# Layer 0 of a two-layer trunk on one core: the norm's factor moved from the tokens to the results, half of a gate product split, later norm tokens, equal address differences

## The chip, the cores and the metric

One Trainium2 chip, one core. The time is device microseconds of one execution, the median over the runs shown. The core's engines are TensorE (PE in the rows; its weight loads are PEld), VectorE (DVE), ScalarE (ACT), GpSimd (POOL) and SyncE (SP), which issues the loads.

## The reference, cut to what matters

`x` is 256 tokens of 1024 float32. Each layer normalizes the tokens, forms one wide projection, feeds branches of width 512, multiplies each with a SiLU gate and adds an output projection to `x`. Layer 0, which the change is about:

```python
h = x * rsqrt(mean(x*x) + EPS) * norm_g[0]             # per token
u_val, u_gate, z_a, q_b, k_b, v_b, z_b = split(h @ e_w_in[0])   # 7 x 512 columns
y_a = conformer_conv(u_val, u_gate, ...) * silu(z_a)   # gated, 31 causal taps, LayerNorm, silu
q = rmsnorm(heads(q_b)); k = rmsnorm(heads(k_b)); v = heads(v_b)
y_b = moba_attention(q, k, v) * silu(z_b)
x = x + concat(y_a, y_b) @ w_out[0]
```

Layer 1 has two other attention branches (c and d) of the same form. The factor rsqrt(...) is one number per token, so it can be multiplied onto the tokens ahead of a product or onto the product's result. A later RMSNorm over a head cancels it but for its EPS.

## The kernel before, in words

A product with fp32 precision is made of three fp32r products: weights and tokens are each split into a high half (`hi`, `hhi`; a cast, mostly on ACT) and a low half (`lo`, `hlo`; the difference, on VectorE, some on POOL), and `mm3` adds hi x hi, hi x lo and lo x hi in one bank. Weights come in quarters of 256 rows (`load_w`: one load, one `hi`, one `lo` of 128 x 1024 each). `proj_chan` puts output channels on the partitions (256 tokens in a row): ug, uv, zb, za, and in layer 1 cc, zc, zd. `proj_tok` puts tokens there (512 columns in a row): qb, kb, vb and others. The first of all products, ug (the convolution's gate), is not split: whole fp32 weights times `h32` (x transposed, times norm_g, not yet the factor), in two passes each.

Layer 0 goes like this. x^T comes in pieces (`h`), is scaled by norm_g, and the ug product starts on it. x itself comes as two blocks of 128 tokens; `first_block` sums the squares, takes the factor by a power on POOL (`rsx`), makes a diagonal (`dg`), and a matmul with ones (`ps_r`) turns it into a row over all partitions (`rb`). `ht` is the scaled x^T, `hhi` and `hlo` its halves. The gate is sg = tanh(ug x rb / 2), and hc = (sg + 1) x uv is the convolution's input. VectorE adds its 31 taps for four groups of channels in turn in two banks (`acc_m`, `acc_o`; 31 x 4 operations), the last of each giving `ya`. `ps_y` transposes `ya` for the LayerNorm, `ps_n` transposes it back. Beside this run the q, k and v products, the attention, and the gates zb and za (`silu2`: tanh on ACT, then z on VectorE). `po` is the output projection with weights `hi_o`, `lo_o`.

No loop sets the order. A Recorder collects every instruction (all of them bear line L384, so rows are told apart by tile names), and `issue` sorts them by the time at which inputs and engine are free, then by the rank of their stage in the table ORDER, then within the stage; for `copy` and `minus` it also picks the engine. Each engine runs its list strictly in order. Loads go out on SP in program order.

## Time and profile before

| | |
|---|---|
| median of 3 runs | 270.2 us (269.99 to 270.39) |
| the profiled execution | 270.53 us, its span 268.5 us |
| granted TensorE clock | 1.0 in each stretch read here |
| busy: PE, DVE, ACT, POOL | 260.0, 197.1, 172.3, 108.0 us |

A row of the timeline gives start, duration, engine, instruction (output<-inputs), and in brackets the idle time of the engine ahead of it with what ended it. Rows of one group run on ("x24" is 24 instructions). Instructions of one engine overlap: the distance of starts, not the duration, is what one costs. In the table by stretch each engine has its busy time and, in brackets, its number of instructions, then come the clock (1.00 is the full level), the DMA share and GB/s.

### The profile page before, as it was taken

How to read it: one execution, taken by the hardware profiler on the slowest of the kernel's cores; microseconds unless marked ns; L12 is line 12 of the kernel's file. 1: busy time of each engine (PE TensorE's matmuls, PEld its weight loads, DVE VectorE, ACT ScalarE, POOL GpSimd, SP SyncE). 2: the span in 40 equal slices, each digit the busy share in tenths (PEclk: the TensorE clock that was granted, in tenths of full speed). 3: DMA queues.
4: the chain of work that ended last, by engine and by line, in shares of the span. 5: the costliest groups of instructions: out<-in, count | busy, mean ns of one | idle time of the engine just before them, and what ended most of it. 6: DMA issues, size and time to landing. Idle time of an engine off the chain costs nothing.

```text
span 268.5 us, 5004 instructions
## 1 busy us (share of the span) xinstructions
PE 260.0 (97%) x1693; PEld 212.4 (79%) x1693; DVE 197.1 (73%) x511; ACT 172.3 (64%) x458; POOL 108.0 (40%) x143
## 2 busy tenths in 40 slices
PE   7889999999999999999899999999999999999994
PEld 5679987878789988878679879678878987667684
DVE  1399999999999999458987213589979856765231
ACT  2267779799995656656467223688869768775300
POOL 0100019858735923202424474154991420545000
PEclk9999999999999999999999999999999999999999
DMA  6998987725763445301858827498885200000031
GB/s 198 361 386 286 354 279 279 212 101 160 236 193 121 171 147 145 89 0 40 282 158 221 231 67 250 160 343 254 273 289 149 86 4 0 2 0 1 2 117 39
DMA packets 28072, 44.89 MB, mean 167 GB/s; under 512 B 3344, under 2 KB 10256, under 8 KB 28048
## 3 DMA queue, kind: packets, MB, share of 16 engines
q1 hardware_dynamic: 28048, 44.58, 50.9%
q8 instruction: 13, 0.21, 0.3%
q14 instruction: 11, 0.09, 0.1%
HBM read 43.26 MB, written 1.05 MB: 165 GB/s over the span
## 4 chain that ended last, share of the span: by engine, by line
PE 61%; DVE 13%; DMA 12%; ACT 5%; POOL 3%; issue 3%; SPq 2%; DVEq 0%; POOLq 0%; ACTq 0%
PE po L384 15%; PE pj_zd L384 5%; PE pj_vb L384 4%; PE pj_za L384 4%; PE pj_zb L384 4%; PE pj_qc L384 4%; PE pj_kv L384 4%; DMA h<-in_prm_dram 3%; PE po_c L384 3%; DMA raw_o<-in_w_out_dram 3%; DMA raw_qd<-in_o_w_in_dram 2%; SPq L384 2%; DMA raw_kb<-in_e_w_in_dram 2%; PE pj_cc L384 2%; PE pt_c L384 2%
## 5 line engine op out<-in xcount | busy, mean ns | idle before, releaser
L384 POOL TENSOR_SCALAR p_c<-p_c,r_c 128x128 f32<-128x128 f32 (+1 forms) x32 | 19.5, 625 | 27.1 <-ACT th_zd L384 8.9
L384 DVE SCALAR_TENSOR_TENSOR acc_m<-hc,cw,acc_m 128x256 f32<-128x256 f32 x58 | 28.0, 483 | 0.2
L384 DVE SCALAR_TENSOR_TENSOR acc_o<-hc,cw,acc_o 128x256 f32<-128x256 f32 x58 | 28.1, 484 | 0.0
L384 PE MATMUL po<-hi_o,yh 128*128 128x512 f32 (+1 forms) x72 | 27.0, 382 | 0.0
L384 PE MATMUL po<-hi_o,yl 128*128 128x512 f32 (+1 forms) x72 | 27.0, 379 | 0.0
L384 PE MATMUL po<-lo_o,yh 128*128 128x512 f32 (+1 forms) x72 | 26.8, 374 | 0.0
L384 POOL TENSOR_TENSOR lo_vb<-raw_vb,hi_vb 128x1024 fp32r<-128x1024 f32 x4 | 9.5, 2409 | 25.7 <-ACT hi_vb L384 25.7
L384 ACT CAST hi_o<-raw_o 128x1024 fp32r<-128x1024 f32 x16 | 16.4, 1045 | 3.4 <-DMA raw_o<-in_w_out_dram 1.6
L384 DVE TENSOR_TENSOR lo_o<-raw_o,hi_o 128x1024 fp32r<-128x1024 f32 x13 | 15.7, 1213 | 1.5 <-ACT hi_o L384 1.5
L384 PE MATMUL pj_ug<-h,raw_ug 128*128 128x256 f32 x64 | 15.4, 392 | 1.4 <-DMA raw_ug<-in_e_w_in_dram 1.4
L384 PEld LDWEIGHTS po<-hi_o,yl 128*128 128x128 f32 x72 | 13.5, 188 | 2.9 <-issue 0.7
L384 ACT ACTIVATE p_c<-sn,mn_c 128x256 f32<-128x256 f32 (+1 forms) x32 | 14.3, 450 | 2.2 <-DVE mn_c L384 2.2
L384 PEld LDWEIGHTS po<-hi_o,yh 128*128 128x128 f32 x72 | 13.6, 189 | 2.7 <-issue 0.3
L384 PEld LDWEIGHTS pj_ug<-h,raw_ug 128*128 128x128 f32 x64 | 12.2, 197 | 3.8 <-issue 2.3
L384 PEld LDWEIGHTS po<-lo_o,yh 128*128 128x128 f32 x72 | 13.6, 188 | 1.9
L384 POOL TENSOR_TENSOR rsx<-ssx,mhalf 128x1 f32<-128x1 f32 x4 | 2.7, 680 | 27.0 <-DVE ssx L384 27.0
L384 DVE TENSOR_TENSOR x<-x,po 128x512 f32<-128x512 f32 (+1 forms) x9 | 5.6, 625 | 8.6 <-PE po L384 8.6
L384 DVE CUSTOM_DVE_ANT_0 sn<-s_c,shp 128x256 f32<-128x256 f32 (+1 forms) x32 | 10.7, 349 | 1.6 <-ACT p_c L384 0.9
L384 POOL TENSOR_TENSOR lo_o<-raw_o,hi_o 128x1024 fp32r<-128x1024 f32 x3 | 7.2, 2417 | 7.0 <-ACT hi_o L384 7.0
L384 PE MATMUL pj_zd<-hlo,hi_zd 128*128 128x256 f32 x32 | 9.4, 295 | 0.0
L384 POOL TENSOR_SCALAR p_b<-p_b,r_b 128x128 f32<-128x128 f32 (+1 forms) x16 | 8.6, 555 | 1.9 <-DVE r_b L384 1.5
L384 PE MATMUL pj_zc<-hhi,lo_zc 128*128 128x256 f32 x32 | 9.2, 287 | 0.2 <-DVE lo_zc L384 0.2
(334 smaller groups left out, 916.5 us busy)
## 6 DMA issues: line engine op xcount, KB each, us to landing
raw_o<-in_w_out_dram SPq DMA_DIRECT2D x16, 512.0 KB, 5.1
raw_uv<-in_e_w_in_dram SPq DMA_DIRECT2D x4, 512.0 KB, 8.3
raw_qb<-in_e_w_in_dram SPq DMA_DIRECT2D x4, 512.0 KB, 5.4
raw_kb<-in_e_w_in_dram SPq DMA_DIRECT2D x4, 512.0 KB, 5.8
raw_vb<-in_e_w_in_dram SPq DMA_DIRECT2D x4, 512.0 KB, 4.7
raw_zb<-in_e_w_in_dram SPq DMA_DIRECT2D x4, 512.0 KB, 4.5
raw_za<-in_e_w_in_dram SPq DMA_DIRECT2D x4, 512.0 KB, 3.6
raw_kv<-in_o_w_in_dram SPq DMA_DIRECT2D x4, 512.0 KB, 3.7
```

The lines of the kernel that those rows point to most:

```text
L384: getattr(self.real[e], method)(*args, **kw)
```

## The change

Layer 0's products take unscaled tokens: `hhi` and `hlo` are the halves of x^T x norm_g, made from eight pieces of 256 columns as these come, and `ht`, the big multiplication by `rb`, is gone. `rb` is multiplied onto results: sg gets a second operation (tanh + 1) x rb, zb and za a multiplication by `rb` ahead of the tanh. In q and k the factor is left in and the head norm's EPS is scaled (`tok`, two small POOL operations per block of tokens); v is scaled by `tok` in its copy. The second half of ug (input rows 512 to 1023) is done with split weights like all others. x's two blocks are loaded after the first uv quarter instead of ahead of h4-7 and the second half of ug. All split tiles get pitches such that the two operands of a product start at equal distances modulo 256 bytes. And ORDER is another table of the same kind.

```diff
...
-ORDER = ["attc 11", "attb 0", "w kv 0", "za 3", "uv", "w uv 1", "pvd 0", "w zd 1", "o1 10", "pvc 31", "pvc 11",
+ORDER = ["w kv 1", "ug", "kd 0", "ln 2", "vb 0", "attd 0", "attb 1", "qd 0", "qd 1", "ln", "zb 1", "norm1 1",
...
-SHIFT = 8
+SHIFT = 48
+CHANNEL_MAJOR = ("uv", "zb", "za", "cc", "zc", "zd")
...
-            whole = name == "ug"
+            whole = name == "ug" and q < 2
             if whole:
-                if q % 2 == 0:
-                    both = act.tile([P, 4, 512], F32, tag=("yh", "yl")[q // 2], name=f"raw_{name}{q}")
+                if q == 0:
+                    both = act.tile([P, 4, 512], F32, tag="yh", name=f"raw_{name}{q}")
...
             if name == "ug" and q == 2:
+                load_xt(4, 4)
+            if name == "uv" and q == 1:
                 for b in range(NB):
...
-                load_xt(4, 4)
...
-            hi = wts.tile([P, 2, 512 + SHIFT], F32R, tag="hi", bufs=PARTS, name=f"hi_{name}{q}")
-            lo = wts.tile([P, 2, 512 + SHIFT], F32R, tag="lo", bufs=PARTS, name=f"lo_{name}{q}")
+            at = SHIFT if name in CHANNEL_MAJOR else 0
+            hi, lo = (wts.tile([P, 1088], F32R, tag=t, bufs=PARTS, name=f"{t}_{name}{q}")[:, at:at + 1024]
+                      .rearrange("p (c f) -> p c f", c=2) for t in ("hi", "lo"))
...
-    def rstd_of(ss, n, scale, name):
+    def rstd_of(ss, n, scale, name, eps=EPS):
...
-        nc.gpsimd.tensor_scalar(out=ms[:p_, :n], in0=ss, scalar1=scale, scalar2=EPS, op0=OP.mult, op1=OP.add)
+        nc.gpsimd.tensor_scalar(out=ms[:p_, :n], in0=ss, scalar1=scale, scalar2=eps, op0=OP.mult, op1=OP.add)
         rs = work.tile([P, 16], F32, tag="rs", name=f"rs_{name}")
...
-    hhi = act.tile([P, KC, S + SHIFT], F32R, name="hhi")[:, :, :S]
-    hlo = act.tile([P, KC, S + SHIFT], F32R, name="hlo")[:, :, :S]
+    hhi = act.tile([P, KC, S], F32R, name="hhi")
+    hlo = act.tile([P, KC, S], F32R, name="hlo")
...
-        return rs
+        return ss[:, 0:1], rs
...
-    hall = gh[:, KC:].rearrange("p (c t) -> p c t", c=KC)
+    tok = [work.tile([P, 2], F32, tag="tok", name=f"tok{b}") for b in range(NB)]
...
     def first_block(b):
...
-        t = slice(b * P, (b + 1) * P)
-        rs = square_sum(b, f"0{b}", ht)
+        ss, rs = square_sum(b, f"0{b}", ht)
...
         nc.tensor.matmul(pr[:, :P], ones, dg, start=True, stop=True)
-        nc.copy(rb[:, t], pr[:, :P])
-        h = ht.rearrange("p q (c t) -> p (q c) t", c=4)
-        nc.stage(f"norm0 r{b}")
-        kw = dict(out=h, in0=hall[:, :, t], in1=rb[:, None, t].to_broadcast([P, KC, P]), op=OP.mult)
-        nc.record(("DVE", "tensor_tensor", (), kw), ("POOL", "tensor_tensor", (), kw), kind="minus")
-        nc.copy(hhi[:, :, t], h)
-        nc.minus(hlo[:, :, t], h, hhi[:, :, t].bitcast(F32))
+        nc.copy(rb[:, b * P:(b + 1) * P], pr[:, :P])
+        nc.gpsimd.tensor_scalar(out=tok[b][:, 0:1], in0=rs, scalar1=ROOT, scalar2=None, op0=OP.mult)
+        nc.gpsimd.tensor_scalar(out=tok[b][:, 1:2], in0=ss, scalar1=EPS / D, scalar2=None, op0=OP.mult)
...
-        rs = square_sum(b, f"1{b}", ht)
+        _, rs = square_sum(b, f"1{b}", ht)
         for q in range(2):
...
             if lo is None:
-                nc.tensor.matmul(ps[:, :S], hi[:, k % 2, f], h32[k], start=k == 0, stop=k == KC - 1)
+                nc.tensor.matmul(ps[:, :S], hi[:, k % 2, f], h32[k], start=k == 0, stop=False)
...
-    def silu2(ps, dst, name):
+    def silu2(ps, dst, name, by=None):
...
         t = work.tile([P, S], F32, tag="tanh", bufs=2, name=f"th_{name}")
-        nc.scalar.activation(t, ps[:, :S], AF.Tanh, scale=0.5)
-        nc.vector.scalar_tensor_tensor(out=dst, in0=t, scalar=1.0, in1=ps[:, :S], op0=OP.add, op1=OP.mult)
+        z = ps[:, :S]
+        if by is not None:
+            nc.vector.tensor_tensor(out=dst, in0=z, in1=by, op=OP.mult)
+            z = dst
+        nc.scalar.activation(t, z, AF.Tanh, scale=0.5)
+        nc.vector.scalar_tensor_tensor(out=dst, in0=t, scalar=1.0, in1=z, op0=OP.add, op1=OP.mult)
...
-    def head_rstd(ps, nh, name):
+    def head_rstd(ps, nh, name, eps=EPS):
...
-            return rstd_of(ss[:, :nh], nh, 1.0 / HD, name)
+            return rstd_of(ss[:, :nh], nh, 1.0 / HD, name, eps)
...
-        return rstd_of(ss[:, :nh], nh, 1.0 / HD, name)
-    def head_norm(ps, name):
+        return rstd_of(ss[:, :nh], nh, 1.0 / HD, name, eps)
+    def head_norm(ps, name, eps=EPS):
...
-        rs = head_rstd(ps, NH, name)
+        rs = head_rstd(ps, NH, name, eps)
         if name[:2] in HEADS_ON_ACT:
...
-        qn = work.tile([P, 256], F32, tag="qd2", bufs=2, name=f"qn_{name}")
+        qn = work.tile([P, 256], F32, tag="tanh", bufs=2, name=f"qn_{name}")
...
     for c in range(KC):
-        nc.either(h32[c], h32[c], ng[:, c:c + 1])
+        by = ng[:, c:c + 1]
+        if c < 4:
+            nc.either(h32[c], h32[c], by)
+        else:
+            nc.scalar.mul(hhi[:, c], h32[c], by)
+            nc.vector.scalar_tensor_tensor(out=hlo[:, c], in0=h32[c], scalar=by, in1=hhi[:, c].bitcast(F32), op0=OP.mult,
+                                           op1=OP.subtract)
+    nc.stage("norm0 g1")
+    for c in range(4):
+        nc.copy(hhi[:, c], h32[c])
+        nc.minus(hlo[:, c], h32[c], hhi[:, c].bitcast(F32))
+    wuv = load_w("uv", [cols_of(0, 0, 512)])
     for b in range(NB):
...
     for m in range(4):
+        nc.stage("ug")
         ps = proj_chan(w, m, "ug")
...
+        nc.vector.scalar_tensor_tensor(out=sg[:, m], in0=sg[:, m], scalar=1.0, in1=rb, op0=OP.add, op1=OP.mult)
...
-    w = load_w("uv", [cols_of(0, 0, 512)])
     for m in range(4):
-        ps = proj_chan(w, m, "uv")
-        nc.vector.scalar_tensor_tensor(out=hc[:, m, PADC:], in0=sg[:, m], scalar=1.0, in1=ps[:, :S],
-                                       op0=OP.add, op1=OP.mult)
+        ps = proj_chan(wuv, m, "uv")
+        nc.vector.tensor_tensor(out=hc[:, m, PADC:], in0=sg[:, m], in1=ps[:, :S], op=OP.mult)
...
-        qn.append(head_norm(proj_tok(w, b, 512, "qb"), f"qb{b}"))
+        qn.append(head_norm(proj_tok(w, b, 512, "qb"), f"qb{b}", tok[b][:, 1:2]))
     w = load_w("kb", [cols_of(0, 2048, 512)])
...
-        kn.append(head_norm(proj_tok(w, b, 512, "kb"), f"kb{b}"))
+        kn.append(head_norm(proj_tok(w, b, 512, "kb"), f"kb{b}", tok[b][:, 1:2]))
...
         ps = proj_tok(w, b, 512, "vb")
-        nc.copy(v0[:, b], ps)
+        nc.scaled(v0[:, b], ps, tok[b][:, 0:1])
...
-        silu2(proj_chan(w, m, "zb"), z[:, 4 + m], f"zb{m}")
+        silu2(proj_chan(w, m, "zb"), z[:, 4 + m], f"zb{m}", rb)
     w = load_w("za", [cols_of(0, 1024, 512)])
...
-        silu2(proj_chan(w, m, "za"), z[:, m], f"za{m}")
+        silu2(proj_chan(w, m, "za"), z[:, m], f"za{m}", rb)
...
-    vcb = act.tile([P, NH, HD], F32, name="vcb")
+    vcb = work.tile([P, NH, HD], F32, tag="qk", name="vcb")
...
```

The order of VectorE around the gate products sg and the uv weights' low halves, first in the kernel before (`sg`, `hlo`, `lo_uv` as above, the rest are small constants):

```order
L384 TENSOR_TENSOR sg_206<-pj_ug_4_108,rb_177 128x256
L384 TENSOR_TENSOR sg_206<-pj_ug_5_115,rb_177 128x256
L384 TENSOR_SCALAR q_c_qnorm_g_213<-shp_121,prm_118 128x4
L384 TENSOR_SCALAR gcmp_215<-shp_121,prm_118 128x4
L384 TENSOR_SCALAR q_d_qnorm_g_217<-shp_121,prm_118 128x4
L384 TENSOR_TENSOR hlo_199<-ht_9_159,hhi_186 128x8x128
L384 TENSOR_TENSOR sg_206<-pj_ug_6_130,rb_177 128x256
L384 TENSOR_TENSOR lo_uv_2_232<-raw_uv_1_123,hi_uv_1_210 128x2x512
L384 TENSOR_TENSOR lo_uv_4_241<-raw_uv_2_128,hi_uv_3_226 128x2x512
L384 TENSOR_TENSOR sg_206<-pj_ug_7_137,rb_177 128x256
L384 TENSOR_TENSOR lo_uv_6_259<-raw_uv_3_132,hi_uv_5_238 128x2x512
L384 TENSOR_TENSOR lo_uv_8_274<-raw_uv_4_135,hi_uv_7_251 128x2x512
```

And in the changed kernel:

```order
L384 TENSOR_TENSOR sg_280<-pj_ug_4_112,rb_261 128x256
L384 TENSOR_TENSOR sg_280<-pj_ug_6_137,rb_261 128x256
L384 TENSOR_TENSOR sg_280<-pj_ug_5_119,rb_261 128x256
L384 SCALAR_TENSOR_TENSOR sg_280<-sg_280,rb_261 128x256
L384 TENSOR_TENSOR sg_280<-pj_ug_7_147,rb_261 128x256
L384 SCALAR_TENSOR_TENSOR sg_280<-sg_280,rb_261 128x256 x3
L384 TENSOR_SCALAR q_b_qnorm_g_315<-shp_140,prm_135 128x4
L384 TENSOR_SCALAR q_c_qnorm_g_318<-shp_140,prm_135 128x4
L384 TENSOR_SCALAR gcmp_321<-shp_140,prm_135 128x4
L384 TENSOR_SCALAR q_d_qnorm_g_324<-shp_140,prm_135 128x4
L384 TENSOR_TENSOR lo_uv_10_327<-raw_uv_5_130,hi_uv_9_268 128x1024
L384 TENSOR_TENSOR lo_uv_12_337<-raw_uv_6_184,hi_uv_11_306 128x1024
```

In the first list two low halves of uv (`lo_uv_2`, `lo_uv_4`) stand between gate products, and the third (`lo_uv_6`) follows the last gate product. In the second the third low half (`lo_uv_10`) comes behind eight gate operations and four constants; `hlo` is made far ahead.

The order of TensorE where the convolution's output is transposed (`ps_y`), before:

```order
L384 MATMUL pj_za_26_1235<-hhi_186,lo_za_46_921 128x256
L384 MATMUL pj_za_26_1235<-hhi_186,hi_za_45_902 128x256
L384 MATMUL po_58_1338<-hi_o_61_1325,yh_15_1193 128x512
L384 MATMUL po_59_1341<-hi_o_61_1325,yh_15_1193 128x512
L384 MATMUL ps_y_52_1343<-ident_110,ya_1129 128x128
L384 MATMUL pj_za_26_1235<-hlo_199,hi_za_45_902 128x256
L384 MATMUL pj_za_26_1235<-hhi_186,lo_za_46_921 128x256
L384 MATMUL ps_y_52_1343<-ident_110,ya_1129 128x128 x3
L384 MATMUL ps_y_53_1356<-ident_110,ya_1129 128x128 x4
L384 MATMUL pj_za_26_1235<-hhi_186,hi_za_47_924 128x256
```

And in the changed kernel:

```order
L384 MATMUL po_59_1404<-hi_o_65_1381,yl_15_1073 128x512
L384 MATMUL po_59_1404<-hi_o_65_1381,yh_14_1065 128x512
L384 MATMUL po_59_1404<-lo_o_66_1396,yh_14_1065 128x512
L384 MATMUL po_59_1404<-hi_o_65_1381,yl_15_1073 128x512
L384 MATMUL ps_y_52_1429<-ident_125,ya_1206 128x128
L384 MATMUL ps_y_53_1432<-ident_125,ya_1206 128x128
L384 MATMUL po_59_1404<-hi_o_67_1394,yh_14_1065 128x512
L384 MATMUL ps_y_52_1429<-ident_125,ya_1206 128x128
L384 MATMUL ps_y_53_1432<-ident_125,ya_1206 128x128
L384 MATMUL ps_y_52_1429<-ident_125,ya_1206 128x128
```

Before, products of the third piece of za stand around and behind `ps_y`; in the changed order they are all done and output products (`po`) stand ahead of it.

The order of VectorE ahead of the last `ya`, before:

```order
L384 SCALAR_TENSOR_TENSOR acc_m_310<-hc_87,cw_191,acc_m_310 128x256 x4
L384 SCALAR_TENSOR_TENSOR z_14_873<-th_za_35_1277,pj_za_27_1238 128x256
L384 SCALAR_TENSOR_TENSOR acc_m_310<-hc_87,cw_191,acc_m_310 128x256 x3
L384 SCALAR_TENSOR_TENSOR y_b_87_1307<-po_b_51_1294,z_14_873 128x256
L384 TENSOR_TENSOR lo_o_60_1314<-raw_o_30_1005,hi_o_59_1299 128x2x512
L384 TENSOR_TENSOR yl_16_1217<-y_b_87_1307,yh_15_1193 128x256
L384 SCALAR_TENSOR_TENSOR ya_1129<-hc_87,cw_191,acc_m_310 128x256 x2
L384 SCALAR_TENSOR_TENSOR y_b_74_1345<-po_b_45_1320,z_14_873 128x256
```

And in the changed kernel:

```order
L384 SCALAR_TENSOR_TENSOR acc_m_374<-hc_79,cw_270,acc_m_374 128x256 x2
L384 SCALAR_TENSOR_TENSOR y_b_76_1341<-po_b_45_1323,z_13_971 128x256
L384 SCALAR_TENSOR_TENSOR acc_m_374<-hc_79,cw_270,acc_m_374 128x256 x3
L384 SCALAR_TENSOR_TENSOR z_13_971<-th_za_35_1328,z_13_971 128x256
L384 TENSOR_TENSOR lo_o_64_1374<-raw_o_32_1000,hi_o_63_1353 128x1024
L384 SCALAR_TENSOR_TENSOR acc_m_374<-hc_79,cw_270,acc_m_374 128x256
L384 TENSOR_TENSOR lo_o_66_1396<-raw_o_33_1135,hi_o_65_1381 128x1024
L384 SCALAR_TENSOR_TENSOR acc_m_374<-hc_79,cw_270,acc_m_374 128x256
L384 SCALAR_TENSOR_TENSOR y_b_89_1418<-po_b_51_1386,z_13_971 128x256
L384 SCALAR_TENSOR_TENSOR ya_1206<-hc_79,cw_270,acc_m_374 128x256 x2
L384 TENSOR_TENSOR z_13_971<-pj_za_27_1336,rb_261 128x256
L384 TENSOR_TENSOR z_13_971<-pj_za_26_1269,rb_261 128x256
```

The multiplication z<-pj_za,rb is new, and two `lo_o` stand close ahead of `ya`, where there was one, with `yl` gone from there and two further multiplications z<-pj_za,rb behind it.

## Rows read from the trace of the kernel before

**Rows 1.** The page, part 1: busy time and share of each engine.

```profile
PE 260.0 (97%) x1693; PEld 212.4 (79%) x1693; DVE 197.1 (73%) x511; ACT 172.3 (64%) x458; POOL 108.0 (40%) x143
```

**Rows 2.** Busy time of each engine by stretch, busy time with instruction count, PE to POOL.

```profile
13.50:34.00 20.50, 19.49 (x133) 18.10 (x134) 19.49 (x35) 15.49 (x23) 0.41 (x1) 1.00 0.97 342
...
80.00:103.00 23.00, 23.00 (x194) 20.69 (x193) 22.69 (x62) 13.71 (x33) 12.21 (x17) 1.00 0.40 134
103.00:124.00 21.00, 21.00 (x106) 16.99 (x105) 14.00 (x31) 12.89 (x23) 4.54 (x6) 1.00 0.26 75
...
200.00:268.50 68.50, 65.08 (x489) 51.79 (x487) 39.64 (x146) 39.72 (x126) 18.94 (x41) 1.00 0.12 42
```

**Rows 3.** Waits of DVE, 13.5 to 103.2 us: us, times, longest.

```profile
DVE lo_qb L384 <- ACT hi_qb L384: 0.5, 2, 0.3
DVE ht L384 <- ACT rb L384: 0.4, 1, 0.4
DVE h L384 <- DMA h<-in_prm_dram: 0.4, 1, 0.4
```

**Rows 4.** Timeline around the convolution's end: start, us, engine, instruction, idle time before.

```profile
90.82 0.19 PEld L384 LDWEIGHTS pj_za<-hhi,hi_za 128*128 128x128 f32 x1 [0.17 <-issue]
...
91.40 0.41 DVE L384 SCALAR_TENSOR_TENSOR z<-th_za,pj_za 128x256 f32<-128x256 f32 x1
...
91.73 0.42 DVE L384 SCALAR_TENSOR_TENSOR y_b<-po_b,z 128x256 f32<-128x256 f32 x1
...
100.88 1.23 DVE L384 TENSOR_TENSOR lo_o<-raw_o,hi_o 128x1024 fp32r<-128x1024 f32 x1
...
102.02 0.42 DVE L384 TENSOR_TENSOR yl<-y_b,yh 128x256 fp32r<-128x256 f32 x1
...
102.35 0.86 DVE L384 SCALAR_TENSOR_TENSOR ya<-hc,cw,acc_m 128x256 f32<-128x256 f32 x2
...
103.13 0.27 PE L384 MATMUL ps_y<-ident,ya 128*128 128x128 f32 x1
```

**Rows 5.** Timeline of the start, and one small POOL operation from later.

```profile
9.71 3.69 PE L384 MATMUL pj_ug<-h,raw_ug 128*128 128x256 f32 x16 [0.93 <-DMA raw_ug<-in_e_w_in_dram]
...
10.88 0.69 DVE L384 CUSTOM_DVE_ANT_0 ht<-x 128x512 f32<-128x512 f32 x1 [3.26 <-DMA x<-in_x_dram]
...
12.19 0.69 DVE L384 CUSTOM_DVE_ANT_0 ht<-x 128x512 f32<-128x512 f32 x1 [0.34 <-DMA x<-in_x_dram]
...
13.23 0.67 POOL L384 TENSOR_TENSOR rsx<-ssx,mhalf 128x1 f32<-128x1 f32 x1 [0.73 <-DVE ssx L384]
...
14.15 0.49 PE L384 MATMUL ps_r<-dg,ones 128*128 128x128 f32 x2 [0.75 <-DVE dg L384]
14.27 0.28 DVE L384 TENSOR_SCALAR dg<-ident,rsx 128x128 f32<-128x128 f32 x1
...
14.99 0.49 PE L384 MATMUL ps_r<-dg,ones 128*128 128x128 f32 x2 [0.35 <-ACT rb L384]
...
15.32 5.34 PE L384 MATMUL pj_ug<-h,raw_ug 128*128 128x256 f32 x24
15.52 0.27 ACT L384 COPY rb<-ps_r 128x128 f32<-128x128 f32 x1 [0.58 <-PE ps_r L384]
...
18.92 0.76 DVE L384 TENSOR_TENSOR sg<-pj_ug,rb 128x256 f32<-128x256 f32 x2
...
24.05 2.35 DVE L384 TENSOR_TENSOR lo_uv<-raw_uv,hi_uv 128x1024 fp32r<-128x1024 f32 x2
...
51.19 0.20 POOL L384 TENSOR_SCALAR ms_qb<-ss_qb 128x8 f32<-128x8 f32 x1
```

**Rows 6.** The chain that ended last, in order of time: start, us, work.

```profile
81.31 5.29 PE pj_zb L384 x43
...
95.30 2.94 PE pj_za L384 x25
...
148.92 11.15 PE pj_qc L384 x48
```

22 rows, old and new, of the table ORDER are left out of this document.

## The prediction

> **What bounds the kernel now.** I read the page first. TensorE is busy 97% of the 268.5 us span and VectorE 73% [rows 1], so at first sight TensorE alone sets the time and whatever shortens its list is a gain. The second view, busy time by stretch, corrects this: VectorE's 73% is an average of full and idle stretches. From 13.5 to 103 us VectorE is as full as TensorE (19.49 of the first 20.5 us, still 22.69 of the last 23), and only from 103 on does it have room (14.00 of 21) [rows 2]. The third view, VectorE's waits from 13.5 to 103.2 us, shows three short ones, 1.3 us in 90 [rows 3]. So in layer 0 VectorE never rests: it writes the low halves of the split weights and adds up the 31 taps of the convolution, and the end of that, the two `ya` at 102.35 to 103.21 us, is where the convolution's output can be transposed (ps_y, 103.13 us on TensorE) and normalized [rows 4]. In the kernel before both engines reach that point together: one `ps_y` starts at 103.13 with no idle time shown ahead of it. Two lines of work therefore end there, and the later one decides. Behind it TensorE alone carries the rest: 21.00 of 21 us up to 124.
>
> The profiled execution took 270.53 us, 2.0 more than its span; the median shown is 270.2. I work out a difference in the span and add it to the median.
>
> **VectorE's line, its start.** The change orders the loads otherwise: after the second ug quarter come h4-7, two ug quarters and the first uv quarter, and only then the two halves of x. The trace has x at 10.88 and 12.19, so 1.31 us for 512 KB, and the ug quarter at 9.71 [rows 5]. Six such loads later x1 is there at 9.71 + 6 x 1.31 = 17.6 us (before: 12.19). From x1's arrival to the start of its power on POOL took 1.04 us (12.19 to 13.23). In the new order VectorE sums both blocks before either power can start, so both powers (0.67 each) stand one behind the other, with two new small scale operations (`tok`) between them. The power on one column takes 0.67 and another scale operation on a few columns, `ms_qb`, 0.20 [rows 5]; the two tok cost 0.4 by the nearer row, 1.3 by the farther. That makes 17.6 + 1.2 + 0.67 + 0.4 + 0.67 = 20.5, where 1.2 is the 1.04 and a second addition of 0.16. From the diagonal (14.27) to the factor row `rb` being copied (15.52 + 0.27) took 1.5 us, which makes about 22.0. Then VectorE scales the gate products: four multiplications and four new (tanh + 1) x rb, 8 x 0.38 (two took 0.76) = 3.0. Eight small constants from prm and shp stand ahead of them and behind them, most of 4 columns; the nearest row, a diagonal of 128 columns at 0.28, would make 2.2 of them, and I take 0.8. That is 22.0 + 3.0 + 0.8 = 25.8 us. Only behind all of these does the list have the third uv quarter's low half; it started at 24.05 before [rows 5]. So VectorE is 1.75 us late there. Bounds: 24.05, if x's later arrival cost nothing, and 26.7 with tok at the farther row. TensorE is stopped behind the same row (it has done 28 uv products by then), but that stop costs only what TensorE cannot recover before `ps_y`.
>
> **VectorE's line, from there to `ya`.** Counted in the order of both kernels, between the third uv low half and `ya`: six multiplications z<-pj,rb are new (four for zb, two for za ahead of the point), one z product less, one y_b more, one yl less, and five lo_o stand ahead instead of three. A 256-column operation here takes 0.33 (91.40 to 91.73) and a lo_o 1.14 (100.88 to 102.02) [rows 4]. 5 x 0.33 + 2 x 1.14 = 3.9 us. Nothing hides this, because VectorE has no idle time to fill [rows 3]. If the two lo_o were moved at no cost (they are done anyway, later, where VectorE has room) it is still 1.65. So `ya` ends 1.75 + 3.9 = 5.65 us later, at 108.9; bounds 105 and 110.5.
>
> **TensorE's line.** The gate product: 32 fp32 passes at 0.2225 (5.34 / 24) become 48 split products at 0.118 [rows 5, 6]: 7.1 less 5.7 = -1.4. The waits on the factor's diagonal and copy, 0.75 and 0.35 [rows 5], go, since both now stand behind all gate products. Against it the stop at the third uv quarter: TensorE reaches it about 2.5 us before its low half is written. Eight za products and five output products stand ahead of `ps_y` instead of behind it: 8 x 0.118 + 5 x 0.232 = 2.1. So TensorE comes to `ps_y` at about 103.1 - 1.4 - 1.1 + 2.5 + 2.1 = 105.2, and waits there for VectorE until 108.9. Behind the point it has 2.1 less to do.
>
> **What follows `ps_y`.** Layer 1 has the same instructions in another order. Instructions of TensorE that carry a wait fall from 174 to 163 there. One that carries a wait starts with 0.17 us idle ahead of it that the trace puts down to issue [rows 4]: between 0 and 11 x 0.17 = 1.9; I take 1.3, since some of these waits coincide with a change of shape that costs the same. The reordering itself can give or cost: TensorE's idle time from 200 us on is 3.4 of 68.5 [rows 2], the output's tail in it, and the stretches before have little, so 1.5 us either way, taken as nothing. VectorE's hlo and norm work behind the point is unchanged.
>
> **Equal address differences.** The trace does not show an address as such. Bounds: 256-column products run at 5.29 / 43 = 0.123 and 2.94 / 25 = 0.1176, 512-column ones at 11.15 / 48 = 0.232 [rows 6]. Of the first 240 stand behind the point, of the second some 350; the spread of the first would be 1.3 us if it were all addresses, and below the best rows nothing is seen. I take 1 ns for a 256-column and 1 ns for a 512-column product, 0.6 us behind the point; ahead of it a shorter TensorE only waits longer. [...]
>
> **Sum.** +5.65 - 2.1 - 1.3 - 0.6 = +1.65 us: span 270.2, and 270.2 + 1.65 = 271.9 for the time. Its own range, from the bounds above, is 270 to 273.5.
>
> **Rivals.**
> TensorE alone decides: VectorE's end is not what `ps_y` waits for, because the planner has other work to put there or VectorE's new operations overlap more than 0.33 each. For it: 97% busy and the common arrival at 103. Against: 1.3 us of VectorE waits in 90. Time: 270.2 - 1.4 - 1.1 - 1.3 - 1.0 (addresses over the whole span) = 265.4 without the uv stop, 267.9 with all of it. I take 266.5: faster.
>
> Mostly given back: `ya` is late only by the 1.65 and some 2 us at the start (the lo_o go behind other work, tok costs nothing), about 3.7 in all; less 2.1, 1.3 and 0.6 it is -0.3, 269.9. For it: the same numbers at their lower bounds.
>
> Addresses do more: the change of pitch brings products clearly below the best rows. [...]
>
> Worse: the uv stop delays hc and with it the convolution's taps, and layer 1's order costs its 1.5: +3 to +4, 273.7.
>
> **How the numbers follow.** A measurement of this kernel can tell 0.2%, 0.54 us, from no change. Forecast 0.52 (slower 0.45, same 0.07); mostly given back 0.18 (faster 0.08, same 0.10); TensorE alone 0.15, faster; addresses 0.07, faster; worse 0.08, slower. Faster 0.30, same 0.17, slower 0.53. The range 266.6 to 273.7 leaves out about half of the TensorE rival and half of the worst case.
>
> **What would show it.** Right: the third uv low half starts near 25.8 and TensorE idles 2 us or more ahead of a pj_uv; `ya` ends near 109; a `ps_y` has idle time released by VectorE; VectorE's waits up to there stay near 1 us. Wrong: `ya` before 106, or no idle time ahead of `ps_y`; rows of pj_zc, po or qc clearly under 0.1176 or 0.232; `rb` copied before 20 us.

## The result, and the profile after

The changed kernel takes 277.99 us (275.1 to 279.26), the kernel before 270.29 on the same chip: a ratio of 1.0262, interval 1.0225 to 1.0299. Forecast were 271.9 us and a range of 266.6 to 273.7: the direction held, the size did not, +7.7 us for +1.7. The profiled execution took 278.9 us. Ratios, and from here on medians, leave out executions over 1.5% above the fastest of their kernel: 279.26 here, which leaves a median of 277.08, and one each of e1, e2 and e8, which the recorded expectations still count (276.6 for e2).

The page of the changed kernel, part 1 [rows 1], and busy time by stretch in the same columns as [rows 2]; the last row begins at its first `ps_y`:

```profile
PE 262.1 (95%) x1709; PEld 214.5 (77%) x1709; DVE 203.5 (73%) x528; ACT 173.9 (63%) x464; POOL 111.4 (40%) x146
```

```profile
13.50:34.00 20.50, 18.56 (x146) 17.69 (x145) 18.89 (x40) 14.99 (x23) 3.00 (x6) 1.00 0.94 320
80.00:103.00 23.00, 19.74 (x164) 17.60 (x165) 23.00 (x60) 11.64 (x29) 8.01 (x14) 1.00 0.51 161
103.00:124.00 21.00, 21.00 (x134) 17.64 (x133) 16.88 (x44) 14.60 (x32) 8.45 (x13) 1.00 0.27 77
...
112.50:276.90 164.40, 158.02 (x1069) 126.78 (x1067) 104.80 (x291) 94.48 (x245) 65.32 (x96) 1.00 0.40 128
```

For the last row, the same stretch of the kernel before, from its first `ps_y` to the end:

```profile
103.10:268.50 165.40, 160.42 (x1082) 129.08 (x1080) 105.86 (x289) 97.41 (x246) 63.88 (x97) 1.00 0.41 130
```

VectorE is now full from 80 to 103 us (23.00 of 23), and TensorE, full there before, idles 3.3 us. The loss lies ahead of `ps_y`: it starts at 112.50 for 103.13 [rows 4], 9.4 us later. Behind it only 1.0 of the 4.0 us forecast came back (165.4 to 164.4): TensorE is busy 2.4 less with 13 products fewer, about the moved work, and idle 1.4 more.

The start, changed kernel, timeline [rows 5]:

```profile
16.06 0.63 ACT L384 ACTIVATE ht<-x 128x512 f32<-128x512 f32 x1 [0.23 <-DMA x<-in_x_dram]
...
17.38 0.63 ACT L384 ACTIVATE ht<-x 128x512 f32<-128x512 f32 x1 [0.59 <-DMA x<-in_x_dram]
...
21.62 0.27 ACT L384 COPY rb<-ps_r 128x128 f32<-128x128 f32 x1
...
22.01 1.08 DVE L384 TENSOR_TENSOR sg<-pj_ug,rb 128x256 f32<-128x256 f32 x3
...
22.48 0.39 PE L384 MATMUL pj_uv<-hhi,hi_uv 128*128 128x256 f32 x1 [1.16 <-DVE sg L384]
...
25.21 2.34 DVE L384 TENSOR_TENSOR lo_uv<-raw_uv,hi_uv 128x1024 fp32r<-128x1024 f32 x2
```

x1 lands at 17.38 (forecast 17.6), `rb` is written at 21.9 (22.0), the third uv low half starts at 25.21 (25.8; before 24.05). What I had not seen is the 1.16 us of TensorE at 22.48: the first uv product goes into a bank from which `sg` has yet to be read. TensorE's stop at a uv low half, forecast at 2.5 us, came to 0.4. Around the convolution's end [rows 4], changed kernel:

```profile
92.69 2.50 POOL L384 TENSOR_TENSOR lo_o<-raw_o,hi_o 128x1024 fp32r<-128x1024 f32 x1 [8.83 <-ACT hi_o L384]
92.90 2.58 DVE L384 SCALAR_TENSOR_TENSOR z<-th_zb,z 128x256 f32<-128x256 f32 x1
...
96.26 0.39 PE L384 MATMUL pj_za<-hhi,hi_za 128*128 128x256 f32 x1 [2.60 <-DVE z L384]
...
111.65 0.86 DVE L384 SCALAR_TENSOR_TENSOR ya<-hc,cw,acc_m 128x256 f32<-128x256 f32 x2
...
112.50 0.38 PE L384 MATMUL ps_y<-ident,ya 128*128 128x128 f32 x2
```

A product of 256 columns takes 2.58 us where its like took 0.41 [rows 4]. It ends just after GpSimd's `lo_o` does (95.48 and 95.19), and TensorE waits 2.60 us behind it. Ahead of `ps_y` itself no idle time is shown. Before, `z<-th_zb,pj_zb` had one input in SBUF and one in PSUM; now the factor is multiplied on first and both inputs, `th_zb` and `z`, are in SBUF. The kernel before had the same neighbours and no stall, as its timeline shows (the first row is two `lo_o`, 2.4 us each):

```profile
85.52 4.80 POOL L384 TENSOR_TENSOR lo_o<-raw_o,hi_o 128x1024 fp32r<-128x1024 f32 x2 [2.32 <-ACT hi_o L384]
...
89.46 0.42 DVE L384 SCALAR_TENSOR_TENSOR z<-th_zb,pj_zb 128x256 f32<-128x256 f32 x1
```

Side by side: the product with both inputs in SBUF takes 2.58 us beside a `lo_o` of 2.50 and ends 0.29 behind it, and the one with an input in PSUM takes 0.42 beside the 4.80. My reading of these rows, put to the test in e8 and e10, was that the first waits out GpSimd's `lo_o`, whose two inputs (`raw_o`, `hi_o`) are in SBUF as well.

VectorE's waits from 25 to 112.5 us [rows 3], and the granted clock (third number from the end) around TensorE's wait of 2.01 us for `qn_qb` at 47.22, both of this execution:

```profile
DVE lo_zb L384 <- ACT hi_zb L384: 2.5, 1, 2.5
DVE acc_o L384 <- ACT acc_o L384: 0.7, 1, 0.7
```

```profile
46.00:48.00 2.00, 0.78 (x5) 0.60 (x5) 2.00 (x6) 1.43 (x6) 2.00 (x2) 0.94 0.63 230
48.00:50.00 2.00, 2.00 (x7) 1.62 (x6) 2.00 (x6) 2.00 (x5) 2.00 (x2) 0.50 0.00 1
50.00:52.00 2.00, 2.00 (x8) 1.57 (x7) 2.00 (x6) 2.00 (x18) 2.00 (x2) 0.70 0.86 260
```

Behind that wait TensorE works at 0.50 and then at 0.70. Then the key products are late, ScalarE's order brings `hi_zb` late, and VectorE, which had no slack, waits 2.5 us.

### The profile page after: what moved, and what is told of

Read it like the earlier page. It is cut to its first block, busy times and chain, and to the rows that moved or that the text cites. A ratio compares the mean times of both kernels' runs of the same rounds, so it can differ in the third digit from the quotient of the medians.

```text
span 276.9 us, 5059 instructions
## 1 busy us (share of the span) xinstructions
PE 262.1 (95%) x1709; PEld 214.5 (77%) x1709; DVE 203.5 (73%) x528; ACT 173.9 (63%) x464; POOL 111.4 (40%) x146
## 4 chain that ended last, share of the span: by engine, by line
PE 56%; DVE 19%; DMA 7%; POOL 7%; ACT 5%; issue 4%; SPq 2%; DVEq 0%; POOLq 0%; ACTq 0%
PE po L384 15%; PE pj_zd L384 4%; PE pj_qc L384 4%; PE pj_za L384 3%; DMA raw_uv<-in_e_w_in_dram 3%; DVE acc_o L384 3%; DVE acc_m L384 3%; PE po_c L384 2%; PE pj_kb L384 2%; PE pj_kd L384 2%; PE pj_kv L384 2%; POOL p_c L384 2%; PE pj_zc L384 2%; PE pj_zb L384 2%; PE pj_cc L384 2%
## 5 line engine op out<-in xcount | busy, mean ns | idle before, releaser
L384 POOL TENSOR_SCALAR p_c<-p_c,r_c 128x128 f32<-128x128 f32 (+1 forms) x32 | 20.9, 670 | 27.0 <-DVE dn L384 14.9
L384 PE MATMUL po<-hi_o,yl 128*128 128x512 f32 (+1 forms) x72 | 26.2, 372 | 0.0
L384 POOL TENSOR_TENSOR lo_o<-raw_o,hi_o 128x1024 fp32r<-128x1024 f32 x3 | 8.1, 2695 | 12.0 <-ACT hi_o L384 12.0
L384 PE MATMUL pj_za<-hhi,hi_za 128*128 128x256 f32 x32 | 9.4, 294 | 2.6 <-DVE z L384 2.6
L384 POOL TENSOR_SCALAR p_d<-p_d,r_d 128x128 f32<-128x128 f32 (+1 forms) x16 | 6.6, 431 | 10.1 <-ACT p_d L384 3.7
L384 PE MATMUL pj_ug<-h,raw_ug 128*128 128x256 f32 x32 | 10.3, 489 | 0.2 <-DMA raw_ug<-in_e_w_in_dram 0.2
L384 PE MATMUL pj_uv<-hhi,hi_uv 128*128 128x256 f32 x32 | 9.1, 286 | 1.2 <-DVE sg L384 1.2
L384 PE MATMUL pt_c<-ident,p_c 128*128 128x128 f32 x48 | 8.8, 282 | 1.3 <-POOL p_c L384 1.3
```

Source lines behind the costliest of these rows:

```text
L384: getattr(self.real[e], method)(*args, **kw)
```

## The experiments

All kernels below are the changed one with its order edited where it is issued, nothing planned anew except in e1. Times are medians of 3 to 6 runs, with the ratio to the kernel before and its interval in brackets. The unedited changed kernel, run again beside the first of them, took 278.07 us (277.63 to 278.57), ratio 1.0296 (1.0248 to 1.0344).

> The changed kernel once more, unedited, to compare the others with on the same chip. Theory A (late head norm: TensorE idles 2 us ahead of the first ps_qk, its clock falls to the lower level, the k products come late, ACT and then VectorE wait): executions with a mean clock of 0.992 to 0.993 take 277 to 279 us and one without a fall about 275; the profile shows the idle time ahead of ps_qk whenever a stretch of lower clock follows. Theory B (VectorE's added operations alone, 3.9 us of them counted): a single value near 278, whatever the clock.

**The wait at 47 us (e2, e7).** One edit moves the waiting transposes, the other fills the gap ahead of them.

```diff
 TensorE, e2:
-ps_qk0<-qn_qb0, ps_qk1<-qn_qb0      (ahead of the first key block)
 pj_kb0<-...                          (24 products)
+ps_qk0<-qn_qb0, ps_qk1<-qn_qb0
 TensorE, e7:
+16 products of 256 columns into ps_qk0's bank, overwritten next
 ps_qk0<-qn_qb0
```

> The changed kernel with one move on TensorE: the two ps_qk transposes that take the first q block stand behind the 24 products of the first k block instead of ahead of them. Nothing is left out. Theory A: no idle time there, clock 1.0 in every execution, VectorE's wait for hi_zb (2.5 us) under 0.7, median 272.5 to 274.5 us, ya about 3 to 4 us earlier. Theory B: the wait turns up elsewhere on TensorE, ya stays near 112, median within 1 us of the unedited one.

> The changed kernel with 16 extra products of 256 columns (0.12 us each, 1.9 in all) into the bank of the first ps_qk right ahead of its first transpose, which overwrites them: the wait for the head norm stays, but TensorE works through it. Theory A with the clock as its larger part: clock 1.0 in every execution, median 274.5 to 276, the fall's 2 to 4 us gone though TensorE still passes the place no earlier than 47 us. Theory A with the wait itself as the larger part: within 1 us of the unedited one. Theory B: within 1 us or slower.

276.31 us (1.0234, 1.0187 to 1.0281) and 276.42 (1.0246, 1.018 to 1.0313), both profiled at a mean clock of 1.0 (e7: 0.999); `ps_y` at 110.4 and 110.2. So some 1.7 us may lie here, less than theory A's 3.6 to 5.6 for e2 and between what the theories gave for e7, and the intervals overlap with the unedited kernel's. Two other executions of e2 had a mean clock of 0.992 and took 276.14 and 276.89, no longer than the profiled one. In the second trace of the unedited kernel that wait did not come at all, its clock fell elsewhere (0.72 and 0.50 at 22 to 26 us, 0.64 and 0.50 again at 94 to 98), and the time was the same, so theory A's sign, idle time ahead of ps_qk wherever the clock is lower, did not hold. The place changes from one execution to the next; over 6 us are still there when this one is taken away.

**Old addresses (e1).** `hi` and `lo` with rows of 520 columns and 8 columns behind each row of `hhi` and `hlo`, as before the change.

```diff
-hi, lo = (wts.tile([P, 1088], ...)[:, at:at + 1024].rearrange("p (c f) -> p c f", c=2) for t in ("hi", "lo"))
+hi = wts.tile([P, 2, 512 + 8], ...)
+lo = wts.tile([P, 2, 512 + 8], ...)
-hhi = act.tile([P, KC, S], ...)                      (hlo alike)
+hhi = act.tile([P, KC, S + 8], ...)[:, :, :S]
```

> The changed kernel with the pitches of the kernel before for hi, lo, hhi and hlo (520 and 264 words), same order of instructions. Theory A: addresses are no part of the loss, 275 to 279 us, within 1 us of the unedited one; the medians of 256-column products stay at 118 ns and of 512-column ones go from 227 back to 231 to 232, which is 350 x 4 ns = 1.4 us at most. Rival C (the new addresses themselves cost): 2 us or more faster.

279.63 us (1.039, 1.0315 to 1.0466), outside both. The time says nothing on addresses: the planner ordered layer 1 anew, and TensorE waits 2.4 us there for `hlo` and 1.6 for `hhi`. The pace of the 512-column products does, the changed kernel first, then e1 (the chain that ended last, as in [rows 6]):

```profile
156.60 7.06 PE pj_qc L384 x31
```

```profile
157.03 11.18 PE pj_qc L384 x48
```

That is 0.228 us a product in the changed kernel and 0.233 with the old pitches, where the kernel before had 0.232 [rows 6]. In layer 0, whose order e1 keeps, the qb products go from 0.227 to 0.233 (45 starts in each trace). So the 512-column products do run about 5 ns faster at the new pitches. The 256-column ones are taken up in e21.

**The product that stalls (e8, e10).** One VectorE step moved by one place.

```diff
 VectorE:
 lo_o001, lo_o002
+z<-th_zb2,z
 lo_o003
-z<-th_zb2,z
```

> The changed kernel with one VectorE step moved: the product z<-th_zb,z of the third zb channel group stands ahead of the last of three lo_o differences instead of behind it, so that it no longer falls beside GpSimd's lo_o (90.6 to 93.1 in the profile of the kernel with the late query transposes). Nothing is left out. Theory (two engines that both read SBUF twice wait for each other): this step falls from 2.58 us to 0.41, TensorE's wait of 2.6 us at a pj_za product goes, the last ya ends 2.0 to 2.2 us earlier, no fall of the clock behind it; 274.6 to 275.9 us against 278.07 of the unedited changed kernel. Rival (the step is long for another reason, or only the number of VectorE's steps counts): it is over 2 us long at its new place too, or the time is won but lost again ahead of ps_y; 277.5 to 278.5 us.

> Both moves together: the two query transposes behind the first key block's products, and the z step out of the way of GpSimd's lo_o. Nothing is left out. Theory (two separate losses): 276.6 of the late transposes less 2.0 to 2.4, 274.2 to 274.8 us, ya ended at 108 to 108.5, the granted clock 1.0 in the profile. Rival (both moves take away the same fall of the clock): 275.5 to 276.6 us.

e8: 274.47 us (1.0172, 1.0127 to 1.0217). e10, both edits: 274.41 (1.0156, 1.0119 to 1.0194), `ps_y` at 107.8, where e2 had 110.4. The four `z<-th_zb,z` in the changed kernel, then in e16 below, which has the edits of e10 and a filling at the start (total, mean ns of one):

```profile
L384 DVE SCALAR_TENSOR_TENSOR z<-th_zb,z 128x256 f32<-128x256 f32 x4 | 3.8, 955 | 0.0
```

```profile
L384 DVE SCALAR_TENSOR_TENSOR z<-th_zb,z 128x256 f32<-128x256 f32 x4 | 1.7, 415 | 0.0
```

The theory of the clash holds in the numbers it gave: 2.2 us less VectorE, 2.6 us earlier at `ps_y`, 3.6 us in the time of e8. That the two losses are separate is not shown: against 278.07 e2 alone gives 1.8 us, e8 alone 3.6, and both together 3.7.

**The start (e9, e15, e16).** e9 loads x and `ident` ahead of `raw_uv0` and puts the scaling of the gate ahead of the second uv low half. e15 leaves the order and fills TensorE's waits there; e16 is e10 with that filling.

```diff
 SyncE, e9:
-raw_uv0, x0, x1, ident
+x0, x1, ident, raw_uv0
 TensorE, e15 and e16:
+6 products of 256 columns into acc_o's bank, which is written anew later
 ps_r1
+9 products of 256 columns into acc_o's bank
 pj_uv0
```

> The changed kernel with the first norm's inputs earlier: the two x blocks and ident are loaded ahead of raw_uv0, ScalarE's and VectorE's work on x stands ahead of the split of raw_uv0, and three of the four products sg<-pj_ug,rb stand ahead of the second uv low half. Nothing is left out. Theory (the late norm factor costs the start what the gate stands later, and the time follows): rb is ready at 20.3 +- 0.4 instead of 21.6 to 21.9, the third lo_uv starts 0.8 to 1.2 us earlier, ya ends as much earlier, 276.9 to 277.3 us against 278.07. Rival (the gate's products end at about 21.3 in any case, and the wait for the bank only changes its name): under 0.4 us, 277.7 to 278.3 us.

> The changed kernel with 15 extra products of 256 columns where TensorE waits at the start: six ahead of the second ps_r and nine ahead of the first pj_uv, into the bank of acc_o, which nothing reads before it is written anew. Nothing is left out. In three of the profiles so far the granted clock fell to 0.66 to 0.72 from 21 to 26 us, behind TensorE's waits of 0.75 and 1.26 us there (or 2.05), in the others it stayed at 1.0. Theory (idle time at the start lets the clock fall, and the late uv products then make ScalarE and VectorE late up to lo_zb, 2.5 to 2.8 us): the clock is 1.0 from 21 to 31 us, the spread of the runs shrinks, and the median comes to 275.2 to 276.8 us against 278.07. Rival (the fall is there but VectorE's line sets the end anyway): 277.6 to 278.5 us.

> The late query transposes and the early z step together (274.41 us) with the same 15 extra products at the start. Nothing is left out. Theory (the four runs of that kernel, at clocks of 0.994 to 1.0, held hardly any fall that cost time): 273.8 to 274.5 us, all runs within 0.5 us of each other. Rival (the extra products come in the way of the first norm's ps_r and of uv): 274.8 to 275.5 us.

e9: 278.24 us, no gain. `rb` was written 0.7 us earlier, but the uv low halves moved behind the gate, the third started at 25.86 for 25.21, and TensorE still waited 1.26 us for `sg`: the edit shifted the same VectorE work about, so it prices nothing. e15: 277.10 (276.03 to 277.94), just outside what either theory gave, and its interval (1.0238 to 1.0325) overlaps with the unedited kernel's. Its clock is 1.0 from 20 to 28 us, and the fall that is left stands behind the z stall (clock third from the end; TensorE busy 0.08 of the first 2 us):

```profile
91.00:93.00 2.00, 0.08 (x1) 0.00 (x0) 2.00 (x2) 0.58 (x1) 1.62 (x1) 1.00 0.74 260
93.00:95.00 2.00, 1.31 (x6) 1.32 (x7) 2.00 (x6) 0.84 (x2) 0.00 (x0) 0.57 0.69 164
95.00:97.00 2.00, 2.00 (x11) 1.73 (x11) 1.59 (x5) 1.84 (x7) 0.00 (x0) 0.57 0.58 184
```

With that stall gone too, e16 took 274.16 (273.01 to 275.32) and, in a second set, 273.25 (273.11 to 273.95; 1.0135, 1.0108 to 1.0163): six runs within 0.9 us, clocks 0.998 to 1.0. The spread of the first set, 2.3 us, and the median of the second lie outside what was expected of them. That is 3.9 and 4.8 us less than the unedited change at 278.07. I read e16 as the change without its accidents, and it is still 3.5 us slower than the kernel before (269.78 in that set).

> The kernel with late query transposes, early z step and the 15 extra products once more, as the measure for the two beside it. Nothing is left out. 273.5 to 274.6 us.

**Is VectorE's counted work paid in full (e13, e17, e18)?** e13 is e2, e17 is e16, with the eight multiplications by `rb` cut to 8 columns. e18 is e16 with two differences behind `ya`. In e18, and in e19 further on, loads that stand behind the moved steps move too.

```diff
 VectorE, e13 and e17:
-z = pj * rb            (128 x 256)
+z[:, :8] = pj * rb     (the rest of z is zero)
 VectorE, e18:
-lo_o011, lo_o012
 ya, ya
+lo_o011, lo_o012
 TensorE, e18: po<-lo_o011 x6 behind ps_y
```

> The kernel with the late query transposes, and the eight multiplications z<-pj,rb cut from 256 to 8 columns (the other columns of z stay zero, so most of that scaling and all that hangs on it is left out; every later step runs on these values in the same form). Theory (VectorE's line from the third uv low half to the last ya sets the middle, so that its counted steps are paid for in full): six of the eight stand ahead of the last ya and take 0.08 to 0.1 us instead of 0.33, ya 1.4 to 1.6 us earlier, 275.0 to 275.3 us against 276.6; if the z step then misses GpSimd's lo_o as well, 272.8 to 273.2 us. Rival (TensorE's own work or its new waits set the middle): 276.2 to 276.9 us.

> The kernel with late query transposes, early z step and the 15 extra products, and the eight multiplications z<-pj,rb cut from 256 to 8 columns (most of that scaling is left out, later steps run on zeros in the same form). In the earlier trial of that cut six of them took 0.65 us instead of 2.00 on VectorE, but a fall of the clock at 22 us lay over it. Theory (counted VectorE steps are paid in full at the last ya): 1.3 to 1.5 us less than the same kernel without the cut, near 272.8. Rival (TensorE's waits set the middle): less than 0.4 us.

> The kernel with late query transposes, early z step and the 15 extra products, and the two last lo_o differences that VectorE makes ahead of the last ya moved behind it, with the six po products that need the first of them behind ps_y. Nothing is left out. Theory (these two differences, 2 x 1.14 us, are a term that stands in full in the last ya): ps_y starts 2.2 to 2.4 us earlier, 0.7 to 1.3 us of it goes to the six products that now stand behind ps_y, 272.4 to 273.5 us. Rival (what follows ps_y waits for the same lo_o, and all is given back): 273.9 to 274.6 us.

e13: 279.25 us, worse than without the cut. Its six products took 0.65 us for 2.00, as counted, but its clock fell to 0.69 at 21 to 26 us, TensorE waited 0.91 and 2.10 us for `qn_qb` and `qn_kb`, and VectorE 2.8 for `hi_zb`: the accident outweighed the cut. With the start filled (e17) the time is 273.18, 1.0 us less than the e16 of that set but only 0.1 less than the second, so the time does not show the size. The traces do. From the third uv low half (25.51 in e17, 24.85 in the second e16) to TensorE's last wait ahead of `ps_y`, for VectorE's `z` at a bank of pj_za, e17 takes 65.92 us and e16 66.83: 0.91 less. From that wait to `ps_y` both take 16.24, at a clock of 1.0, as the changed kernel does. Its row, e16's, and that of the second trace of the unedited kernel, where the clock fell in this stretch:

```profile
96.26:112.50 16.24, 16.24 (x130) 14.05 (x130) 16.06 (x48) 12.35 (x33) 5.98 (x12) 1.00 0.45 132
```

```profile
91.68:107.92 16.24, 16.24 (x130) 14.04 (x131) 16.06 (x48) 12.43 (x34) 7.44 (x13) 1.00 0.52 161
```

```profile
94.16:112.02 17.86, 17.86 (x130) 15.34 (x130) 16.32 (x48) 12.54 (x33) 6.08 (x12) 0.90 0.42 119
```

TensorE has no gap there. So the four cut multiplications for zb, ahead of that wait, come back in full at `ps_y` (some 0.23 us saved on each) and the two for za, behind it, not at all; and a fall of the clock in that stretch costs `ps_y` 1.6 us (1.4 in e15, which takes 17.68) while VectorE idles.

e18 took 278.47 (1.0339), 4.3 us worse. `ps_y` did come early, at 106.15, but by 1.5 us of that stretch (81.53 from the third uv low half, for 83.07) where 2.2 to 2.4 were expected: TensorE's part behind its last wait is 1.2 shorter by the moved products, and VectorE waits 1.0 for TensorE's `po_b`. Then:

```profile
105.56 2.37 POOL L384 TENSOR_TENSOR lo_o<-raw_o,hi_o 128x1024 fp32r<-128x1024 f32 x1 [0.43 <-ACT hi_o L384]
105.99 4.68 DVE L384 TENSOR_TENSOR lo_o<-raw_o,hi_o 128x1024 fp32r<-128x1024 f32 x2
...
110.72 0.80 PE L384 MATMUL po<-lo_o,yh 128*128 128x512 f32 x1 [3.54 <-DVE lo_o L384]
```

Neither theory had this. The pair of differences now meets a GpSimd `lo_o` and takes 4.68 us for 2.36: the same clash, made by moving work out of the way. TensorE then waits 3.54 us.

**Behind `ps_y` (e21, e19).** Both are e16 with one edit, run in one set with it.

```diff
 e21 (every engine's order unchanged):
-SHIFT = 48
+SHIFT = 0
 VectorE, e19:
 lo_zd2
-lo_zd3, lo_o100
 z<-th_zc2, kcd
+lo_zd3, lo_o100
```

> The same kernel with SHIFT = 0 instead of 48: the weights of uv, zb, za, cc, zc and zd stand at the start of their tiles, so that the equal address differences of the change are given up for them; every engine's order is the same, word for word. Nothing is left out. Theory of the forecast (equal differences save 0.6 us, its smallest term): 0.3 to 0.9 us slower than the kernel beside it, spread over the products of those weights, their medians up by 1 to 2 ns. Rival (pairs of products cost the same at either address, as the equal mean pitches of the two kernels say: 232 and 232 ns of 512 columns, 118 and 118 of 256): within 0.2 us.

> The same kernel with two VectorE differences of layer 1 (the last lo_zd and the first lo_o) moved about 3 us back, behind kcd, where VectorE sat idle 1.2 and 1.4 us, so that they don't stand back to back with the lo_zd before them while GpSimd's p_c multiplications want to read. Nothing is left out. Theory (the new wait of layer 1, 1.31 us at a pt_c for GpSimd's p_c, is the same clash of two engines): the p_c of 2.60 us ends 1.1 us earlier, the wait falls to 0.2 or less, 0.7 to 1.2 us faster than the kernel beside it. Rival (TensorE meets the next wait, at kcd's or lo_zd's products): within 0.3 us or slower.

e21: 273.71 us (272.54 to 274.53) for 273.25, not told apart by the time. The chain that ended last tells more; three runs of products of the moved weights, with the same count, e16 first:

```profile
145.47 2.47 PE pj_cc L384 x21
...
200.65 2.59 PE pj_zc L384 x22
204.99 2.83 PE pj_zc L384 x24
```

```profile
145.22 2.51 PE pj_cc L384 x21
...
200.79 2.63 PE pj_zc L384 x22
205.17 2.87 PE pj_zc L384 x24
```

0.04 us in each, 1.7 to 1.9 ns a product, so the rival (nothing) is wrong on the pace. Other runs of these weights differ by 0 (`pj_zd` x34, 4.07 us in both) to 0.07, and qc, whose weights did not move, by nothing (x31, 7.06 in both). The kernel before, with other paddings, ran 256-column products at 0.1176 to 0.123 [rows 6], and 2.59 / 22 is 0.1177: for this width the change keeps what was there. For 512 columns the rival's equal 232 ns do not stand: e1 above shows 0.228 after and 0.232 before.

e19: 273.07 us, the rival's number. The mechanism is the theory's, as the rows show, e16 first, then e19:

```profile
194.05 5.76 POOL L384 TENSOR_SCALAR p_c<-p_c,r_c 128x128 f32<-128x128 f32 x4
...
197.19 2.35 DVE L384 TENSOR_TENSOR lo_zd<-raw_zd,hi_zd 128x1024 fp32r<-128x1024 f32 x2
...
199.86 0.33 PE L384 MATMUL pt_c<-ident,p_c 128*128 128x128 f32 x1 [1.31 <-POOL p_c L384]
```

```profile
194.12 5.02 POOL L384 TENSOR_SCALAR p_c<-p_c,r_c 128x128 f32<-128x128 f32 x4 [1.03 <-DVE r_c L384]
...
197.57 1.22 DVE L384 TENSOR_TENSOR lo_zd<-raw_zd,hi_zd 128x1024 fp32r<-128x1024 f32 x1
...
199.19 0.33 PE L384 MATMUL pt_c<-ident,p_c 128*128 128x128 f32 x1 [0.26 <-POOL p_c L384]
```

In e16 one `p_c`, of 2.60 us, waits out two VectorE differences that stand back to back, 2.35 us together: it ends at 199.81, they at 199.54; with the second one gone, TensorE's wait falls from 1.31 to 0.26. It buys next to nothing: TensorE waits 0.5 us for `a_c` at transposes ahead of it, where e16 has no such wait, and loses another half in front of pj_zd. No version found here beats the kernel before.

## Why the prediction was wrong

Its steps against two traces after, in us (e16 is the second set; in brackets what the kernel before has):

| step | forecast | changed kernel | e16 |
|---|---|---|---|
| third uv low half starts (24.05) | +1.75 | +1.16 | +0.80 |
| from there to `ps_y` (79.08) | +3.9 | +8.2 | +4.0 |
| from `ps_y` to the end (165.4) | -4.0 | -1.0 | -2.0 |
| span (268.5) | +1.65 | +8.4 | +2.8 |

The second line by stretch, in the columns of [rows 2]: the kernel before, the changed one, e16.

```profile
24.05:103.13 79.08, 78.93 (x518) 67.21 (x518) 78.19 (x191) 63.22 (x193) 42.35 (x37) 1.00 0.61 200
```

```profile
25.21:112.50 87.29, 81.46 (x524) 69.18 (x522) 83.96 (x199) 64.86 (x193) 42.52 (x38) 0.98 0.55 179
```

```profile
24.85:107.92 83.07, 80.11 (x524) 68.15 (x523) 81.79 (x199) 64.81 (x193) 41.85 (x38) 1.00 0.59 190
```

VectorE is busy 3.6 us more in e16 than before and idle 0.4 more. The changed kernel adds 2.2 of busy time, the product that stalls, and 2.05 of idle time (3.33 for 1.28).

**What held.** VectorE is full up to `ps_y`; the start, as far as one trace can tell it (in e16's first trace the third uv low half starts at 26.55, 1.7 us later than in the second); and the size of the counted work: 4.0 measured for 3.9, once e16 takes the accidents away. That agreement is in part luck, see step 2. `ps_y` there is at 107.9, the forecast was 108.9 (instruction count, shortest, middle and longest in ns, first and last start):

```profile
L384 PE MATMUL ps_y<-ident,ya x8: 272/273/273, 107.9 to 108.9; 128*128 128x128 f32 x8
```

So the rivals "TensorE alone" and "mostly given back" fell, and "worse" (+3.5 through the uv stop and layer 1's order) had the sign but other causes.

**Failed step 1, "from there to `ya`".** I counted six new multiplications and left the z product that follows them at its old 0.33. Its price depends on where its inputs are and on what GpSimd does meanwhile: +2.2 us on VectorE and 2.6 of waiting TensorE. e8 and e10 show it. Going through the added instructions by the memory of each input, with rows of the kernel before, would have found it. There the 0.42 beside a GpSimd `lo_o` has one input in PSUM; a `lo_kv`, with both in SBUF, takes 2.32 beside GpSimd's `lo_cc`, where the other three take 1.22:

```profile
124.16 4.59 DVE L384 TENSOR_TENSOR lo_kv<-raw_kv,hi_kv 128x1024 fp32r<-128x1024 f32 x3
...
126.25 3.65 POOL L384 TENSOR_TENSOR lo_cc<-raw_cc,hi_cc 128x512 fp32r<-128x512 f32 x2 [3.45 <-ACT hi_cc L384]
```

**Failed step 2, TensorE "waits there [at `ps_y`] for VectorE until 108.9", and "VectorE's waits up to there stay near 1 us".** I let TensorE wait at the start and at `ps_y` for free, because VectorE was the bound. But in no trace has the first `ps_y` idle time ahead of it, which the prediction had named as a sign of being wrong. TensorE meets VectorE 16.24 us earlier, at the bank of a pj_za product, and from there to `ps_y` it runs without a gap through the products that the new order puts ahead. Behind that wait both lines are as long as each other, and work taken off VectorE there does not come back (e17, e18); of the counted 3.9 only the four zb multiplications, 4 x 0.33, are shown to be paid at `ps_y`.

Nor were the waits free. In some executions the granted clock fell to 0.50 behind waits of 2.0 and 2.6 us, TensorE became late, and through ScalarE's order VectorE waited 2.5 us. With the waits filled or removed the clock was 1.0 at those places (e15 from 20 to 28 us, the first e16 from 11 to 116; e7 has a mean of 0.999); with the z stall's removal that is the 3.9 to 4.8 us of e16. In the traces of the table it is 2.2 us for the product and 2.05 for VectorE's waiting; in other executions the falls come at other places.

**Failed step 3, "What follows `ps_y`".** Moved work -2.1: busy time fell by 2.4. Fewer waiting instructions -1.3: idle time rose by 1.4 instead, 1.3 of it at one `pt_c` behind the same clash (e19), and taking that away moves the wait on. A count of instructions that carry waits says nothing of how long they wait, and the 0.17 us was no price of a wait. Its row stands right behind a `po_b`, where the shape changes from 128*64 to 128*128, and the same gap stands at other such changes in the kernel before, as below; products of 256 columns that follow their like start 118 ns apart (median) in the changed kernel, with a wait or without.

```profile
102.10 0.19 PEld L384 LDWEIGHTS pj_za<-hhi,hi_za 128*128 128x128 f32 x1 [0.17 <-issue]
```

Addresses -0.6, at 1 ns for either width: against the kernel before the 256-column products won nothing (0.1177 for 0.1176), though their pace does depend on the place of the weights (e21); the 512-column ones won about 5 ns in qc (e1) and 3 in po (4.81 / 21 behind `ps_y`, 5.11 / 22 before), so one sign of being wrong, rows of po or qc clearly under 0.232, came in part. Over some 350 of them that would be 1.0 to 1.8 us, an estimate from these paces; it is not seen in the sum, which the new order and its waits outweigh. That addresses could do more than this was an estimate, and no run shows it.

Open: what lets the clock fall in one execution and not in another behind the same waits, 0.75 and 1.26 us at the start, 2.60 at the z stall; and why e2 and e8 give together no more than e8 alone.

## What to carry to other kernels

When an operand moves from PSUM to SBUF, or a step is split in two, look for VectorE instructions that now read SBUF twice, and for GpSimd work beside them: here the product took 2.58 us for 0.41 and ended 0.29 behind GpSimd's `lo_o`, and moving work made such a clash (4.68 us for 2.36 in e18) as easily as it ended one. Waiting was not free for TensorE even off the bound: what followed 2.01 us of it ran at a clock of 0.50 in the changed kernel and handed the delay back to the engine that was full, as 2.5 us of VectorE's waiting. When two engines are both full up to a point, find the last place where one waits for the other: what was saved behind that place on one of them alone did not come back here (16.24 us from it to `ps_y` in e16 and e17 alike). A forecast from counts of instructions held to 0.1 us here, in part by luck, and only for the kernel in which nothing collided.
